# Maximum along the last axis on one core: 17 loads in place of 18, the first of 16 rows, 41 blocks through GpSimd in place of 38, and the last pieces in multiples of 64 columns

## The chip, the core and the metric

The kernel runs on one core of a Trainium2 chip. The engines that matter here are VectorE (DVE in the profile), which reduces along the free dimension; TensorE (PE), used to transpose; ScalarE (ACT), which copies out of PSUM; GpSimd (POOL), which reduces across partitions; and SyncE (SP), whose queue issues the loads. The metric is the device time of one execution in microseconds. The kernel before has a median of 163.62 us in 3 runs (163.6 to 163.85).

## The reference

```python
def setup_inputs():
    batch, seq, dim = 32, 512, 1024
    return {
        "x": np.random.randn(batch, seq, dim).astype(np.float32),
    }

def reference(x: np.ndarray) -> np.ndarray:
    return np.max(x, axis=-1).astype(np.float32)
```

There are 32x512 = 16384 rows of 1024 float32 values, 67.1 MB in all. The output has one value for each row, 64 KB in all.

## The kernel before

The 16384 rows are spread over 128 partitions, so each partition holds 128 rows of 1024 columns. "A row" below always means one such row on all 128 partitions, 512 KB. `BLOCKS` (lines 13 to 16) cuts the 128 rows into loads. The first list is one region of x of 112 rows per partition; the second is a region of 16 rows, 14 of them in loads and 2 in pieces. Each load is one DMA of n rows.

All loads go into a ring of 47 rows in SBUF (`ring`, line 66), whose first 128 columns hold the results (`res`). A load that doesn't fit before the ring's end starts again at row 0. A load is issued from SP's queue (`issue`, line 231) only when every reader of the rows that it overwrites has been written into the program, and on the chip it then waits for those readers. Loads also take turns with eight semaphores, so a load waits for the landing of the load eight places ahead of it.

`PLAN` (lines 31 to 34) is the order of the work, written out by hand. All engines follow it: `in_turn` (line 71) chains each engine's instructions in that order. A step is a letter and a number:

- `d` (direct, line 184): one VectorE maximum over the rows of a load that are VectorE's alone.
- `t` (turn, line 152): a chunk of at most eight 128-column blocks goes another way. TensorE transposes each block into PSUM (`ps`), ScalarE copies them to SBUF (`sb`), and GpSimd's all-reduce takes the maximum over partitions (`top`).
- `b` (back, line 172): TensorE turns one partition of `top` back, a 1x128 transpose for each block, into a small PSUM tile: `got`, one for a load, or for loads in `RANK` the tile `joint`, one for all of them.
- `p` (partial, line 190): VectorE's maximum over the columns of a shared row that GpSimd doesn't take, written beside the values of `b` in the same PSUM tile.
- `m` (merge, line 197): VectorE's maximum over the values of one row in `got` or `joint`, which gives the row's result. `m99` merges all of `joint` and is the last reduction.
- `f` (line 266): VectorE's maximum over one piece.

`SHARED` (line 20) says for a load how many of its rows are shared and how many of their blocks GpSimd takes: `10: (3, 8)` gives GpSimd three whole rows of load 10, `13: (2, 3)` three blocks of two rows each. In all that is 24+6+6+2 = 38 blocks. `RANK` (line 22) lists the loads whose shared rows end in `joint` and sorts them to the end of their region.

`turned` (`sb`), `allr` (`top`) and `psum` (`ps`) have two buffers each (lines 59 to 61), and `joint` is one tile in a pool with one buffer (line 128). The framework puts a semaphore wait between any two instructions of different engines that touch the same tile, one of them writing, in the order of the program; it doesn't compare the columns of `joint`. A third chunk's `top` waits until the first chunk's `b` has read that buffer.

The last two rows come in `PIECES` (line 26): two pieces each, 532+492 and 592+432 columns. The first piece of a row leaves its maximum in the column just before the second piece, whose reduction takes it in. Each piece starts at a multiple of 16 columns in the ring (line 212).

After the first direct maximum come ScalarE's table load and GpSimd's first instruction of the body (lines 252 to 256). The results go out in two stores from ScalarE's queue: 112 columns after the first piece's reduction, 16 after `m99` (lines 270 to 273).

Of the kernel before, what the change touches and what calls it, by code (L numbers as in the profile page):

```python
# [8 lines left out]
F32 = mybir.dt.float32  # L9

BLOCKS = [
    [2, 15, 16, 14, 11, 11, 10, 10, 8, 8, 7],
    [3, 3, 3, 2, 1, 1, 1],
]
RING = 47


SHARED = {10: (3, 8), 13: (2, 3), 14: (2, 3), 17: (1, 2)}  # L20

RANK = {13: 1, 14: 2, 17: 2}

PIECES = [(532, 492), (592, 432)]

PLAN = """
    d0 d1 d2 d3 d4 d5 d6 d7 d8 d9 t0 d10 t1 t2 d11 b0 d12 b1 d13 t3 p13 b2 p14 t4 m10 d15 b3
    d16 p17 t5 f0 b4 f1 f2 b5 f3 m99
""".split()

NOSYNC = mybir.DependencyInfo(mybir.DependencyClass.NoSync, mybir.DependencyReason.DATA)
# [4 lines left out]
def kernel(  # L41
# [11 lines left out]
    N, D = xf.shape  # L53
    C = D // P
    I = N // P
# [10 lines left out]
    ring = once.tile([P, I + RING * D], F32)  # L66
    res = ring[:, :I]
# [9 lines left out]
    def maximum(out, in_):  # L77
        return in_turn("DVE", nc.vector.reduce_max(out=out, in_=in_, axis=X))  # L78
# [15 lines left out]

    loads = []
    views = []
    last = len(PIECES)
    first = at = 0
    for sizes in BLOCKS:
        S = sum(sizes) + last * (sizes is BLOCKS[-1])  # L100
        xb = xf[first * P:(first + S) * P, :].rearrange("(p i) d -> p i d", p=P)
# [5 lines left out]
        b, place = 0, {}  # L107
        for i in sorted(range(len(sizes)), key=lambda i: RANK.get(base + i, 0)):
            place[i] = b
# [8 lines left out]
    assert first == I  # L118
    shared = [SHARED.get(j, (0, C)) for j in range(len(loads))]

    lead = [0 if RANK.get(j) == 3 else n - m for j, ((_, n, _, _), (m, _)) in enumerate(zip(loads, shared))]
    final = [j for j in range(len(loads)) if j in RANK]
    final.sort(key=lambda j: loads[j][3])
# [11 lines left out]
    def rows(j):  # L135
        start, n, _, _ = loads[j]
        return ring[:, I + start * D:I + (start + n) * D].rearrange("p (i d) -> p i d", d=D)
# [4 lines left out]
    def share(j):  # L142
        m, parts = shared[j]
        if j in RANK:
            r = loads[j][3] + lead[j] - col0
            return joint[:, r:r + m, :]
        if j not in fetched:
            got = psmall.tile([P, m, parts + (parts < C)], F32)
            fetched[j] = got
        return fetched[j]  # L150
# [39 lines left out]
    def partial(j):  # L190
        m, parts = shared[j]

        s = width - parts if j in RANK else 1
        maximum(share(j)[:, :, parts:], rows(j)[:, lead[j]:lead[j] + m, parts * P:].rearrange(
# [11 lines left out]
    pieces = []  # L206
    tail = []
    room = I + at * D
    for q in range(len(PIECES[0])):
        for r, widths in enumerate(PIECES):  # L210
            c, w = sum(widths[:q]), widths[q]
            room = -(-(room + 1) // 16) * 16
            pieces.append((ring[:, room:room + w], xb[:, S - last + r, c:c + w]))
            if q:
                tail[-last] = (ring[:, room - 1:room], tail[-last][1])
            tail.append((res[:, I - last + r:I - last + r + 1],
                         ring[:, room - (q > 0):room + w]))
            room += w
    assert room <= I + (at + last + 1) * D


# [81 lines left out]
```

## Time and profile before

| what | value |
|---|---|
| time, median of 3 | 163.62 us |
| span of the profiled execution | 162.0 us |
| around the span, to the median | 1.6 us |
| VectorE busy | 135.3 us (84%) |
| GpSimd, ScalarE, TensorE busy | 16.0, 6.3, 13.6 us |
| mean rate of the DMA engines | 415 GB/s |
| load of 2 rows reduced from | 5.49 us |
| first GpSimd all-reduce | 141.9 us |
| last all-reduce ends | 158.6 us |
| joint maximum ends | 159.68 us |

The span runs from the first to the last instruction of the one execution that was profiled; the device time holds some start and end around it as well. Times in the trace count from the span's start. A line of instructions gives the start, the busy time, engine and line of the code, output and input tile, and in brackets the engine's idle time before it and what ended it. Line 78 is the helper for all VectorE maxima, so its instructions are told apart by their shapes.

### The profile page before, as it was taken

The numbers are of one execution on the slowest core, as the hardware profiler recorded it, in microseconds if no ns is written. First come the engines' busy times: TensorE is split into PE (matmuls) and PEld (weight loads), VectorE is DVE, ScalarE is ACT, GpSimd is POOL, SyncE is SP. The second block draws the span as 40 slices with busy tenths as digits, with TensorE's granted clock in tenths as the row PEclk, the third lists the DMA queues.
The fourth block names the chain that finished last, engine by engine and source line by source line (L and its number), as shares of the span: only waits on it lengthen the run. The fifth ranks groups of instructions, "written<-read, shape, count | busy, mean of one in ns | idle before, by whom it ended". The sixth has DMA issues, their size and how long they took to land.

```text
span 162.0 us, 297 instructions
## 1 busy us (share of the span) xinstructions
PE 13.6 (8%) x76; PEld 11.7 (7%) x76; DVE 135.3 (84%) x33; ACT 6.3 (4%) x7; POOL 16.0 (10%) x11
## 2 busy tenths in 40 slices
PE   0000000000000000000000000000000000772942
PEld 0000000000000000000000000000000000762731
DVE  3500019998399999999999999996999999999994
ACT  0020000000000000000000000000000000241120
POOL 0000000000000000000000000000000000099791
PEclk9999999999999999999999999999999999997555
DMA  5996999599789999898999899799999999999991
GB/s 176 569 486 273 455 502 518 259 518 518 326 354 453 453 405 534 356 534 356 434 456 455 354 486 465 344 486 388 429 478 388 424 418 453 395 431 419 412 386 47
DMA packets 3456, 67.18 MB, mean 415 GB/s; under 512 B 640, under 2 KB 896, under 8 KB 1536
## 3 DMA queue, kind: packets, MB, share of 16 engines
q1 hardware_dynamic: 3168, 67.11, 97.0%
q10 hardware_dynamic: 288, 0.07, 0.2%
HBM read 67.11 MB, written 0.07 MB: 415 GB/s over the span
## 4 chain that ended last, share of the span: by engine, by line
DMA 50%; DVE 47%; SPq 1%; issue 0%; DVEq 0%
DMA ring<-in_x_dram 50%; DVE ring L78 45%; DVE joint L78 2%; SPq L238 1%; DVEq L298 0%
## 5 line engine op out<-in xcount | busy, mean ns | idle before, releaser
L78 DVE TENSOR_REDUCE ring<-ring 128x1 f32<-128x1024 f32 (+13 forms) x20 | 130.0, 6548 | 23.4 <-DMA ring<-in_x_dram 23.3
L168 POOL PARTITION_ALL_REDUCE top<-sb x6 | 15.7, 2657 | 135.0 <-ACT sb L166 134.9
L160 PE MATMUL ps<-ident,ring 128*128 128x128 f32 x38 | 9.1, 424 | 139.9 <-DMA ring<-in_x_dram 139.9
L160 PEld LDWEIGHTS ps<-ident,ring 128*128 128x128 f32 x38 | 7.6, 224 | 139.9 <-issue 139.9
L166 ACT COPY sb<-ps 128x1024 f32<-128x1024 f32 (+2 forms) x6 | 5.0, 834 | 143.2 <-PE ps L160 136.2
L78 DVE TENSOR_REDUCE joint<-ring 128x2 f32<-128x1280 f32 (+1 forms) x3 | 3.9, 1314 | 0.0
L178 PE MATMUL got<-ident,top 1*128 1x1 f32 x24 | 2.7, 228 | 3.7 <-POOL top L168 3.6
L178 PEld LDWEIGHTS got<-ident,top 1*128 1x128 f32 x24 | 2.4, 188 | 4.6 <-POOL top L168 4.6
L178 PE MATMUL joint<-ident,top 1*128 1x1 f32 x14 | 2.0, 245 | 1.9 <-POOL top L168 1.9
L178 PEld LDWEIGHTS joint<-ident,top 1*128 1x128 f32 x14 | 1.7, 210 | 2.7 <-POOL top L168 2.7
L166 ACT ACT_TABLE_LOAD x1 | 1.3, 1283 | 7.9 <-DVE ring L78 7.9
L83 DVE MEMSET ident<- 128x128 f32 x1 | 0.2, 165 | 0.8 <-PEq L287 0.8
L255 POOL MEMSET gate<- 128x1 f32 x1 | 0.1, 99 | 7.4 <-DVE ring L78 7.4
L90 DVE TENSOR_SCALAR rowno<-rowno 32x1 f32<-32x1 f32 x3 | 0.4, 146 | 0.1
L85 DVE TENSOR_TENSOR_SCAN colno<-ident 128x128 f32<-128x128 f32 x1 | 0.4, 424 | 0.0
L92 DVE TENSOR_SCALAR ident<-colno,rowno 128x128 f32<-128x128 f32 x1 | 0.3, 288 | 0.0
L87 DVE STREAM_TRANSPOSE rowno<-colno 128x32 f32<-128x32 f32 x1 | 0.2, 213 | 0.0
L78 DVE TENSOR_REDUCE ring<-got 128x3 f32<-128x24 f32 x1 | 0.2, 173 | 0.0
L78 DVE TENSOR_REDUCE ring<-joint 128x5 f32<-128x20 f32 x1 | 0.2, 169 | 0.0
L287 POOL MEMSET const-float32-0.0<- 128x1 f32 x1 | 0.1, 98 | 0.2 <-issue 0.2
L287 POOL MEMSET const-bfloat16-1.0<- 128x1 bf16 x1 | 0.1, 101 | 0.0
L287 POOL MEMSET const-uint8-127<- 128x1 uint8 x1 | 0.1, 101 | 0.0
(2 smaller groups left out, 0.2 us busy)
## 6 DMA issues: line engine op xcount, KB each, us to landing
ring<-in_x_dram SPq DMA_DIRECT2D x2, 5632.0 KB, 29.9
ring<-in_x_dram SPq DMA_DIRECT2D x2, 5120.0 KB, 36.8
ring<-in_x_dram SPq DMA_DIRECT2D x2, 4096.0 KB, 32.5
ring<-in_x_dram SPq DMA_DIRECT2D x1, 7680.0 KB, 22.5
ring<-in_x_dram SPq DMA_DIRECT2D x1, 7168.0 KB, 57.8
ring<-in_x_dram SPq DMA_DIRECT2D x3, 1536.0 KB, 35.7
ring<-in_x_dram SPq DMA_DIRECT2D x1, 3584.0 KB, 29.2
ring<-in_x_dram SPq DMA_DIRECT2D x2, 1024.0 KB, 17.7
```

Source lines behind the costliest of these rows:

```text
L78: return in_turn("DVE", nc.vector.reduce_max(out=out, in_=in_, axis=X))
L83: in_turn("DVE", nc.vector.memset(ident, 1.0))
L85: in_turn("DVE", nc.vector.tensor_tensor_scan(out=colno, data0=ident, data1=ident, initial=-1.0, op0=ALU.add, op1=ALU.mult))
L87: in_turn("DVE", nc.vector.transpose(out=rowno, in_=colno[:, :32]))
L90: in_turn("DVE", nc.vector.tensor_scalar(out=part, in0=part, scalar1=float(q * 32), scalar2=None, op0=ALU.add))
L92: identity = in_turn("DVE", nc.vector.tensor_scalar(out=ident, in0=colno, scalar1=rowno[:, 0:1], scalar2=None, op0=ALU.is_equal))
L160: in_turn("PE", nc.tensor.transpose(out=ps[:, w:w + P], in_=rows(j)[:, lead[j] + r + i, c * P:(c + 1) * P], identity=ident,))
L166: in_turn("ACT", nc.scalar.copy(out=sb[:, :W], in_=ps[:, :W]))
L168: in_turn("POOL", nc.gpsimd.partition_all_reduce(top[:, :W], sb[:, :W], P, bass_isa.ReduceOp.max))
L178: in_turn("PE", nc.tensor.transpose(out=share(j)[:, r + i, c:c + 1], in_=tops[k][0:1, w:w + P], identity=ident[0:1, 0:1],))
L238: load = nc.sync.dma_start(out=rows(issued), in_=src)
L287: nc = _bacc.Bacc("TRN2", target_bir_lowering=False, num_devices=1)
```

## The change

The rows are cut anew: 16, 12, 14, 13, 13, 11, 10, 9, 7, 7 in the first region and 4, 3, 2, 2, 1, 1, 1 and two rows of pieces in the second. That is 17 loads in place of 18, and the first has 16 rows where it had 2. Loads are renumbered by this: load 8 is the seven-row load just ahead of the last one of the first region, and 10 to 16 are the second region's.

GpSimd takes blocks of seven loads: three blocks of a row of load 8, four blocks of each row in four rows of load 9, three of three rows of load 10, three of two rows of load 12, three of a row of load 14, and two of a row of loads 15 and 16. That makes 3+16+9+6+3+2+2 = 41 blocks in nine chunks (before: 38 in six). Loads 10, 12, 14, 15 and 16 end in `joint`, eight rows of four values; loads 8 and 9 have merges of their own (`m8`, `m9`). In the plan each of these loads has a `p` step, and the `b` steps of loads 10, 12 and 14 now stand between the `p` steps of later loads: `p10`, `p12`, `b3`, `b4`, `p14`, `b5`, `p15`, `p16`, `b6`.

Pieces are written as (row, width) in the order of their issue: 640 of the first row, 576 of the second, 384 of the first, 448 of the second. Widths are multiples of 64 columns, and pieces start at multiples of 64 columns in the ring.

```diff
 BLOCKS = [
-    [2, 15, 16, 14, 11, 11, 10, 10, 8, 8, 7],
-    [3, 3, 3, 2, 1, 1, 1],
+    [16, 12, 14, 13, 13, 11, 10, 9, 7, 7],
+    [4, 3, 2, 2, 1, 1, 1],
 ]
 RING = 47
-SHARED = {10: (3, 8), 13: (2, 3), 14: (2, 3), 17: (1, 2)}
-RANK = {13: 1, 14: 2, 17: 2}
-PIECES = [(532, 492), (592, 432)]
+SHARED = {8: (1, 3), 9: (4, 4), 10: (3, 3), 12: (2, 3), 14: (1, 3), 15: (1, 2), 16: (1, 2)}
+RANK = {10: 1, 12: 2, 14: 2, 15: 2, 16: 2}
+PIECES = [(0, 640), (1, 576), (0, 384), (1, 448)]
 PLAN = """
-    d0 d1 d2 d3 d4 d5 d6 d7 d8 d9 t0 d10 t1 t2 d11 b0 d12 b1 d13 t3 p13 b2 p14 t4 m10 d15 b3
-    d16 p17 t5 f0 b4 f1 f2 b5 f3 m99
+    d0 d1 d2 d3 d4 d5 d6 d7 t0 d8 b0 p8 m8 t1 d9 t2 p9 t3 d10 b1 p10 t4 d11 b2 t5 m9 p12 b3
+    b4 d13 t6 p14 b5 p15 t7 p16 t8 b6 f0 f1 b7 f2 f3 b8 m99
 """.split()
...
-    last = len(PIECES)
+    last = 1 + max(r for r, _ in PIECES)
...
-    for q in range(len(PIECES[0])):
-        for r, widths in enumerate(PIECES):
-            c, w = sum(widths[:q]), widths[q]
-            room = -(-(room + 1) // 16) * 16
-            pieces.append((ring[:, room:room + w], xb[:, S - last + r, c:c + w]))
-            if q:
-                tail[-last] = (ring[:, room - 1:room], tail[-last][1])
-            tail.append((res[:, I - last + r:I - last + r + 1],
-                         ring[:, room - (q > 0):room + w]))
-            room += w
+    done = [0] * last
+    before = [None] * last
+    for r, w in PIECES:
+        c, q = done[r], before[r]
+        room = -(-(room + 1) // 64) * 64
+        pieces.append((ring[:, room:room + w], xb[:, S - last + r, c:c + w]))
+        if q is not None:
+            tail[q] = (ring[:, room - 1:room], tail[q][1])
+        before[r] = len(tail)
+        tail.append((res[:, I - last + r:I - last + r + 1], ring[:, room - (q is not None):room + w]))
+        done[r] = c + w
+        room += w
+    assert done == [D] * last
```

## The prediction

> **What bounds the kernel now.** I read the busy times and the queues first, then who waits for whom, the chain, and the last 25 us instruction by instruction.
>
> The page's busy times and queues:
>
> ```profile
> PE 13.6 (8%) x76; PEld 11.7 (7%) x76; DVE 135.3 (84%) x33; ACT 6.3 (4%) x7; POOL 16.0 (10%) x11
> ...
> q1 hardware_dynamic: 3168, 67.11, 97.0%
> ```
>
> Who waits for whom (us, times, longest):
>
> ```profile
> DVE ring L78 <- DMA ring<-in_x_dram: 23.3, 4, 15.8
> ```
>
> The end of the chain in order of time (start, us):
>
> ```profile
> 110.86 38.94 DMA ring<-in_x_dram
> 149.81 0.02 issue
> 149.83 1.22 DVE ring L78
> ...
> 158.42 0.51 DVE ring L78
> 158.92 0.08 issue
> 159.00 0.59 DVE ring L78
> ```
>
> The load queue keeps the DMA engines busy for 97.0% of the span: the kernel streams 67.11 MB and has no hole in the stream. VectorE (DVE) is the second limit. It loses 23.3 us to loads, nearly all before 43 us, and after 110.8 us never again more than some hundredths: blocks shrink so that each lands just as the one before is reduced. The chain ends in both: the last two pieces (158.42, 159.00) start when they land, and 0.6 us later only the joint maximum and a store follow. So the change can win little and lose whatever makes VectorE wait near the end.
>
> The last stage in the timeline (start, us):
>
> ```profile
> 148.38 1.01 PE L178 MATMUL got<-ident,top 1*128 1x1 f32 x8 [2.55 <-POOL top L168]
> ...
> 152.43 2.50 POOL L168 PARTITION_ALL_REDUCE top<-sb  x1 [0.90 <-ACT sb L166]
> ...
> 154.99 0.79 PE L178 MATMUL joint<-ident,top 1*128 1x1 f32 x6 [0.92 <-POOL top L168]
> 155.05 2.50 POOL L168 PARTITION_ALL_REDUCE top<-sb  x1
> 156.26 0.96 DVE L78 TENSOR_REDUCE joint<-ring 128x2 f32<-128x768 f32 x1
> ...
> 158.66 0.37 PE L178 MATMUL joint<-ident,top 1*128 1x1 f32 x2 [0.25 <-POOL top L168]
> 159.51 0.17 DVE L78 TENSOR_REDUCE ring<-joint 128x5 f32<-128x20 f32 x1
> ```
>
> These are durations I use: a 768-column all-reduce on GpSimd 2.50, six transposes back into the joint tile 0.79, two 0.37, a partial maximum over 768 columns 0.96, the final joint maximum (ends 159.68). In the steps d, t, b, p, m, f below (direct maximum, turn and all-reduce, back, partial, merge, piece) the number is a load's for d, p, m, a chunk's for t, b, a piece's for f.
>
> **Loads.** The two-row load was reduced from 5.49, the load that completes 89 rows from 110.82: 105.33 us for 87 rows and seven loads. Pieces were issued at 142.44, 146.13 and 149.82, each at the landing of a three-row load: 3.69 for three rows and one load. So a row costs 1.2045 us and a load 0.076. One load fewer gains 0.08. Landings in the changed kernel: the first 16 rows at 5.47+14x1.2045 = 22.33; 68 rows (load 4) 85.27; load 12 149.72; loads 14, 15, 16 at 153.48, 154.76, 156.04; pieces 156.87, 157.62, 158.15, 158.75. Before, the same sum gives 158.83 for the last piece. Alignment of the pieces to 64 columns touches 2.7 us of transfers (two rows, four loads); the last piece of before lands as the sum has it, so I take nothing, and 0.1 either way at most.
>
> Does the stream stay full? Load 3 waits for d0 (ends 39.6) while loads up to 53.8 are queued; load 5 for d2 (68.9, queued to 85.3); load 8 for d4 (99.3, to 121.7); load 10 for d5 (111.1, to 138.7); the last piece for load 12 (149.7, 8 us ahead of its turn). The smallest margin is 8 us, so SP's moved waits cost nothing.
>
> **VectorE.** The forms give 17.22 us for 16 rows and 1.21 for one: 1.067 a row plus 0.146, and an instruction with nothing to wait for starts 0.085 before the last one ends, so 0.06 net. Three blocks more on GpSimd take 384 columns off: -0.40. Two reductions more (27 against 25), +0.12; m8, p15 and p16 each wait for the reduction just ahead on VectorE, which costs the overlap and 0.03, about 0.11 each. Sum near zero. The late start at 22.3 is no loss either: VectorE still waits for loads 2, 3 and 4 (1.4, 0.7, 1.7), so its time is set by load 4 at 85.3. From there to the end of p12: 56 whole rows 59.75, 5888 columns of partials 6.14, 14 instructions 0.84, m8's wait 0.11, last end 0.09: 152.25. ScalarE's table load and GpSimd's library step move behind the first reduction, to 39.6; first use is after 130.
>
> **GpSimd and its waits.** Nine all-reduces instead of six: two of 1024 columns (3.3 each), two of 768 (2.50), two of 256 (1.12) and three of 384, which no row shows; between 1.12 and 2.50, by length 1.46. About 18.2 us of work from 131 to the end, so it has room. What it lacks is freedom of order. There are two result buffers (top), so t5 may start only when b3 has read t3's; and b3 writes the joint tile, for which the built order makes it wait until p12 has written the same tile. Then b5 waits for t5, and p15, again a writer of the joint tile, waits for b5. In the kernel before, p17 stood behind b3 alone, which ended at 155.78, before its load landed at 156.1; no partial was held up by TensorE.
>
> That loop, step by step: p12 ends 152.25; b3 starts 0.06 later (as 154.99 follows 154.93) and takes 0.79: 153.10. GpSimd starts 0.09 later (152.43 after ScalarE's 152.34): 153.19, and t5 takes 2.50: 155.69. (t5's own input is ready sooner: load 12 lands at 149.72, six transposes 1.5 and a copy 0.80 as at 149.94 and 151.54, 152.2 with hand-overs.) b5: 0.06+0.79: 156.54. p15 starts about 0.04 later: 156.58. Without it, VectorE would have been ready at: d13 from 152.20 (its load) 2.28, p14 0.73, 155.22, and 0.03: 155.25. Load 15 is there at 154.76. So VectorE stands still 1.33 us, with p16, all four pieces and the final maximum queued behind. The DMA runs on underneath; no cover is left, because VectorE was just on time.
>
> After it: p15 0.96, p16 0.03+0.96, four pieces (640, 576, 385, 449 columns) 0.81+0.75+0.55+0.61, joint maximum 0.18, less five overlaps of 0.085: 4.43. End 161.01, against 159.68: **+1.33**. Close beside it runs GpSimd's own end: p16 ends 158.53, b6 0.06+0.48 (three transposes, 0.106 less for each than six), t8 0.09+1.12, b8 0.06+0.37: 160.71, before the joint maximum's 160.83. With 2.50 for each 384 the loop still stands (t4 would end 153.1, as b3 does) and the end moves by under 0.1.
>
> The span is 162.0 and the median 163.62; the 1.62 around the span and the 2.3 from the last maximum to the span's end stay. 163.62+1.33 = **164.95**.
>
> Terms unknown: b3 and b5 at the faster pace of the first transposes (eight in 0.65 at 145.18, against 1.01 at 148.38 after the granted clock went to 0.5) would give back 0.27 each: 164.4. I take the slow pace, since both lie after 147.6, where all rows of before are slow. The step from TensorE to a GpSimd or VectorE instruction that waits for a buffer is not shown; the nearest hand-overs are 0.03 and 0.14 (landing at 156.13, start 156.27), three such in the loop: -0.1 to +0.3.
>
> The Trainium skill, page "PSUM — Partial Sum Buffer", section on bank collisions, has two engines on one bank and quadrant collide whatever bytes they touch, and asks for semaphores by bank, not by address. By it the waits of b3 and p15 on each other's writes are needed, though they touch different columns: 164.95; if columns alone counted, 163.6. No run here shows a collision; the built order has the waits.
>
> **Rivals.**
> *No stall.* The wait is met in time, because t5 or its neighbours run 1.33 us sooner than summed. Then VectorE ends at 161.01-1.33 = 159.68, as before: 163.6, no change. For it: VectorE's work and the last landing are equal to 0.1. Against: two 2.50 rows, and the order of waits is fixed.
> *A load has a large fixed cost.* The first load was issued at 0.72 and landed at 5.47, of which its two rows are 2.41: 2.34 us fixed. If each load paid that in the stream, one load fewer brings every landing forward by it, the loop with them: 164.95-2.34 = 162.6, faster; it decides from 1.7 us per load on. Against: one- and three-row loads follow each other at 0.076. The Trainium skill, page "DMA: Bandwidth & Descriptors", gives about 2.0 us fixed per DMA; by it the time would be 162.95. The trace's 3.69 us for three rows disagrees for queued loads.
> *A second stall.* GpSimd's end takes over: if waits on buffers cost 0.3 each, t5 and t8 together bring 0.4 to 0.6: 165.4.
>
> **Chances.** Forecast with its unknown terms 0.80 (164.4 to 165.3), second stall 0.11, no stall 0.06, fixed cost 0.03. Range 164.3 to 165.45 leaves about 0.1 to 0.15 out. Bound of what can be told is 0.2%, 0.33 us: slower 0.91, same 0.06, faster 0.03.
>
> **What would show it.** VectorE idle about 1.3 us before a 768-column partial into the joint tile at 156.6, ended by TensorE; GpSimd idle about 1.1 us before the second 768-column all-reduce at 153.2; the last piece landed near 158.75 but reduced only from 160.3; joint maximum near 160.8. Wrong if that partial starts at 155.3, if p12 ends well before 152, or if DMA shows holes.

## The result, and the profile after

The changed kernel takes 165.62 us in the median of four runs (165.59 to 165.65). Against the kernel before on the same chip that is a ratio of 1.0116 [1.0103, 1.013]: slower, by about 1.9 us. The forecast was 164.95 us with a range of 164.3 to 165.45, so the direction was right, and the time lies 0.17 us above the range. The profiled execution took 165.61 us, its span is 163.8.

The page of the changed kernel, with the same two parts as shown of before, busy times and load queue:

```profile
PE 15.7 (10%) x82; PEld 12.7 (8%) x82; DVE 135.1 (82%) x35; ACT 7.1 (4%) x10; POOL 18.1 (11%) x14
...
q1 hardware_dynamic: 3024, 67.11, 95.8%
```

VectorE is busy for 135.1 us where it was 135.3: the three blocks more on GpSimd and the two reductions more nearly cancel, as the prediction had it. The queue moves the same 67.11 MB, and its share falls because the span is longer.

The waits of VectorE, total, times, longest:

```profile
DVE ring L74 <- DMA ring<-in_x_dram: 23.9, 4, 20.2
...
DVE joint L74 <- PE joint L174: 1.5, 1, 1.5
```

The second line is new. Before, VectorE never waited for TensorE.

The last stage in the timeline (start, busy time, instructions; in brackets the idle time before and what ended it):

```profile
151.11 1.48 DVE L74 TENSOR_REDUCE joint<-ring 128x2 f32<-128x1280 f32 x1
152.56 2.29 DVE L74 TENSOR_REDUCE ring<-ring 128x2 f32<-128x2048 f32 x1
...
152.74 1.09 PE L174 MATMUL joint<-ident,top 1*128 1x1 f32 x9 [1.04 <-DVE joint L74]
153.68 3.91 POOL L164 PARTITION_ALL_REDUCE top<-sb  x2 [1.23 <-PE joint L174]
...
154.77 0.82 DVE L74 TENSOR_REDUCE joint<-ring 128x1 f32<-128x640 f32 x1
...
156.23 0.79 PE L174 MATMUL joint<-ident,top 1*128 1x1 f32 x6 [1.40 <-POOL top L164]
...
157.06 1.96 DVE L74 TENSOR_REDUCE joint<-ring 128x2 f32<-128x768 f32 x2 [1.48 <-PE joint L174]
...
158.93 2.46 DVE L74 TENSOR_REDUCE ring<-ring 128x1 f32<-128x640 f32 x4
...
160.90 0.37 PE L174 MATMUL joint<-ident,top 1*128 1x1 f32 x2 [1.07 <-POOL top L164]
161.30 0.19 DVE L74 TENSOR_REDUCE ring<-joint 128x8 f32<-128x32 f32 x1
```

Read the brackets from top to bottom: TensorE's `b3` waits for VectorE (`p12`), GpSimd's `t5` for TensorE, `b5` for GpSimd, and VectorE's `p15` for TensorE. This is the loop of the forecast. VectorE had nothing to do from 155.58, where `p14` ends, to 157.06. Then `p15` and `p16`, four pieces without a gap and the joint maximum, which ends 161.50 where it ended 159.68 before.

The chain that ended last, in order of time, goes through the same loop (start, length, what):

```profile
0.72 21.93 DMA ring<-in_x_dram
22.65 0.02 issue
...
85.59 0.02 issue
85.62 52.66 DVE ring L74 x5
...
151.19 1.41 DVE joint L74
...
152.74 0.78 PE joint L174 x6
...
153.68 2.51 POOL top L164
...
156.23 0.81 PE joint L174 x6
...
157.06 0.97 DVE joint L74
```

The first load landed at 22.65 and load 4 at 85.59. In the chain of before the last two pieces followed their landings; here they don't: the last piece landed at 159.03 and was reduced from 160.78.

### The profile page after: what moved, and what is told of

Read it like the earlier page. It is cut to its first block, busy times and chain, and to the rows that moved or that the text cites. A ratio compares the mean times of both kernels' runs of the same rounds, so it can differ in the third digit from the quotient of the medians.

```text
span 163.8 us, 329 instructions
## 1 busy us (share of the span) xinstructions
PE 15.7 (10%) x82; PEld 12.7 (8%) x82; DVE 135.1 (82%) x35; ACT 7.1 (4%) x10; POOL 18.1 (11%) x14
## 3 DMA queue, kind: packets, MB, share of 16 engines
q1 hardware_dynamic: 3024, 67.11, 95.8%
HBM read 67.11 MB, written 0.07 MB: 410 GB/s over the span
## 4 chain that ended last, share of the span: by engine, by line
DVE 61%; DMA 33%; POOL 2%; issue 2%; PE 1%; POOLq 0%
DVE ring L74 56%; DMA ring<-in_x_dram 33%; DVE joint L74 3%; DVE got L74 2%; POOL top L164 2%; PE joint L174 1%; POOLq L164 0%
## 5 line engine op out<-in xcount | busy, mean ns | idle before, releaser
L74 DVE TENSOR_REDUCE ring<-ring 128x13 f32<-128x13312 f32 (+14 forms) x17 | 124.5, 7361 | 23.9 <-DMA ring<-in_x_dram 23.9
L164 POOL PARTITION_ALL_REDUCE top<-sb x9 | 17.8, 2017 | 103.0 <-ACT sb L162 101.3
L156 PE MATMUL ps<-ident,ring 128*128 128x128 f32 x41 | 10.5, 426 | 137.6 <-DMA ring<-in_x_dram 137.5
L162 ACT COPY sb<-ps 128x384 f32<-128x384 f32 (+3 forms) x9 | 5.8, 644 | 111.5 <-PE ps L156 109.2
L74 DVE TENSOR_REDUCE joint<-ring 128x2 f32<-128x768 f32 (+3 forms) x5 | 6.4, 1273 | 1.5 <-PE joint L174 1.5
L174 PE MATMUL joint<-ident,top 1*128 1x1 f32 x22 | 2.9, 241 | 4.6 <-POOL top L164 2.5
L74 DVE TENSOR_REDUCE got<-ring 128x1 f32<-128x640 f32 (+1 forms) x2 | 3.1, 1552 | 0.0
L174 PEld LDWEIGHTS joint<-ident,top 1*128 1x128 f32 x22 | 2.6, 211 | 5.8 <-POOL top L164 4.4
```

The source lines that it names most:

```text
L156: in_turn("PE", nc.tensor.transpose(out=ps[:, w:w + P], in_=rows(j)[:, lead[j] + r + i, c * P:(c + 1) * P], identity=ident,))
L162: in_turn("ACT", nc.scalar.copy(out=sb[:, :W], in_=ps[:, :W]))
L164: in_turn("POOL", nc.gpsimd.partition_all_reduce(top[:, :W], sb[:, :W], P, bass_isa.ReduceOp.max))
L174: in_turn("PE", nc.tensor.transpose(out=share(j)[:, r + i, c:c + 1], in_=tops[k][0:1, w:w + P], identity=ident[0:1, 0:1],))
```

## The experiments

Two theories were set against each other. The first: the loop of waits costs the time. Rivals: more work or a later end on GpSimd (nine all-reduces, 41 blocks), and the first load of 16 rows. Ratios are to the kernel before on the same chip, where its medians were 163.81 to 163.87.

### The loop taken out, all else kept

```diff
-RANK = {10: 1, 12: 2, 14: 2, 15: 2, 16: 2}
+RANK = {12: 2, 14: 2, 15: 2, 16: 2}
...
-    b4 d13 t6 p14 b5 p15 t7 p16 t8 b6 f0 f1 b7 f2 f3 b8 m99
+    b4 d13 t6 m10 p14 p15 t7 p16 t8 b5 b6 f0 f1 b7 f2 f3 b8 m99
...
-        top = allr.tile([P, D], F32)
+        if W <= 256:
+            top = allr2.tile([P, 256], F32)
+        else:
+            top = allr.tile([P, D], F32)
```

(`allr2` is a second pool with two buffers.) Load 10's values go to a tile of their own, so `b3` no longer stands behind `p12`; `b5` moves behind all three partials and `t8`; and the last two chunks have result buffers of their own.

> The changed kernel with all its 41 blocks and nine chunks, but the waits taken away by other buffers and order: load 10's rows get a tile of their own outside joint, chunks t7 and t8 a result buffer of their own, and p14, p15, p16 stand ahead of b5. Theory (the loop p12, b3, t5, b5, p15 costs VectorE 1.4 us): p15 starts right behind p14 at 155.6, the joint maximum ends near 160.05 in place of 161.50, time 165.62-1.45 = 164.2. Rival (it is the GpSimd work itself, 41 blocks and nine chunks, that makes the end late): 165.6 stays.

Measured: 164.18 us (8 runs), ratio 1.0024 [1.0014, 1.0034]. Its last stage:

```profile
152.71 2.50 POOL L168 PARTITION_ALL_REDUCE top<-sb  x1 [0.24 <-ACT sb L163]
...
154.87 2.81 DVE L75 TENSOR_REDUCE joint<-ring 128x1 f32<-128x640 f32 x3
...
157.58 2.46 DVE L75 TENSOR_REDUCE ring<-ring 128x1 f32<-128x640 f32 x4
...
159.96 0.17 DVE L75 TENSOR_REDUCE ring<-joint 128x5 f32<-128x20 f32 x1
```

`t5` now waits for its own input from ScalarE, and the three partials run in one stretch, with no idle time ahead of any. The joint maximum ends 1.37 us sooner and the time falls by 1.44 (by 1.33 against the second set of runs of the changed kernel, further below). All 41 blocks and nine all-reduces are still there, and so is the first load of 16 rows. So the loop is 1.3 to 1.4 of the 1.7 to 1.9 us by which those two sets are slower than before, and the rival on GpSimd's work falls.

### Each half of it alone

Only the order of one step, `p15` ahead of `b5`:

```diff
-    b4 d13 t6 p14 b5 p15 t7 p16 t8 b6 f0 f1 b7 f2 f3 b8 m99
+    b4 d13 t6 p14 p15 t7 b5 p16 t8 b6 f0 f1 b7 f2 f3 b8 m99
```

> The changed kernel with two steps moved: p15 and t7 ahead of b5, so that p15 no longer waits for b5; all else is as it is, b3 still waits for p12. Theory: p15 starts right behind p14 at 155.6, but b5 now stands behind p15 and p16 behind b5, so the wait shrinks and moves: VectorE idle about 0.9 ahead of p16 (starts 157.5 in place of 158.06), joint maximum 161.0 in place of 161.5, time 165.1. Rival (p15's wait is the whole loss): joint maximum 160.1, time 164.2.

Measured: 164.94 us (4 runs), ratio 1.0064 [1.0049, 1.0079].

```profile
153.52 5.06 POOL L164 PARTITION_ALL_REDUCE top<-sb  x3 [1.23 <-PE joint L174]
...
154.61 1.81 DVE L74 TENSOR_REDUCE joint<-ring 128x1 f32<-128x640 f32 x2
...
156.57 0.77 PE L174 MATMUL joint<-ident,top 1*128 1x1 f32 x6 [0.83 <-DVE joint L74]
...
157.38 0.96 DVE L74 TENSOR_REDUCE joint<-ring 128x2 f32<-128x768 f32 x1 [0.95 <-PE joint L174]
```

`t5` still waits for TensorE and so for `p12`, but `p15` runs at once behind `p14`. Now `b5` waits for `p15` and `p16` waits for `b5`.

Only load 10's own tile (line `RANK` as above, `m10` behind `t6`, `b5` left ahead of `p15`):

```diff
-    b4 d13 t6 p14 b5 p15 t7 p16 t8 b6 f0 f1 b7 f2 f3 b8 m99
+    b4 d13 t6 m10 p14 b5 p15 t7 p16 t8 b6 f0 f1 b7 f2 f3 b8 m99
```

> The changed kernel with load 10's three shared rows in a PSUM tile of their own (one merge more), order otherwise unchanged: b3 needs not wait for p12 any more, so t5 starts at 152.7 in place of 153.7. p15 still waits for b5, and b5 for p14. Theory: b5 starts behind p14 at 155.8, VectorE idle about 0.9 ahead of p15 (starts 156.6 in place of 157.06), joint maximum 161.0, time 165.1. Rival (b3's wait for p12 is the whole cause): joint maximum 160.1, time 164.2.

Measured: 165.09 us (4 runs), ratio 1.0074 [1.0059, 1.0089].

```profile
152.52 2.50 POOL L164 PARTITION_ALL_REDUCE top<-sb  x1 [0.23 <-ACT sb L162]
...
155.64 0.77 PE L174 MATMUL joint<-ident,top 1*128 1x1 f32 x6 [0.98 <-DVE joint L74]
...
156.45 1.96 DVE L74 TENSOR_REDUCE joint<-ring 128x2 f32<-128x768 f32 x2 [0.95 <-PE joint L174]
```

`t5` is now 1.16 us sooner than in the changed kernel (153.68), and yet `p15` gains only 0.61: `b5` waits no longer for GpSimd but for `p14`, which writes the same tile. Both halves leave 0.95 us of idle time, and it is the same thing in both: VectorE's partial ends, about 0.15 later TensorE starts six transposes, 0.77, and 0.04 later VectorE may write the tile again. One `b` of six transposes between two adjacent `p` on one tile costs that much, however early its input is. Neither edit alone takes it away. The first experiment, where it is gone, goes further than the two together: `b5` stands behind all three partials, with the extra result buffers that this needs. Whether that order would have been enough without load 10's own tile was not run.

### The same kind of wait put into the kernel before

```diff
-    d16 p17 t5 f0 b4 f1 f2 b5 f3 m99
+    d16 t5 b4 p17 f0 f1 f2 b5 f3 m99
```

> The kernel before with one step moved: p17 behind t5 and b4, so that it waits for TensorE's transposes of chunk 4 into the joint tile, as p15 waits for b5 in the changed kernel. No work is added. Theory (such a wait late in the plan costs its full length, as nothing covers it): p17 starts behind b4 at 158.45 in place of 156.26, joint maximum about 161.8 in place of 159.68, time 163.62+2.1 = 165.7. Rival (a wait of VectorE there is absorbed by the pieces still landing until 158.9): the end moves by under 0.5, time below 164.1.

Measured: 166.03 us (4 runs), ratio 1.0136 [1.0122, 1.0149].

```profile
157.75 0.80 PE L178 MATMUL joint<-ident,top 1*128 1x1 f32 x6 [0.58 <-POOL top L168]
...
158.58 0.96 DVE L78 TENSOR_REDUCE joint<-ring 128x2 f32<-128x768 f32 x1 [2.04 <-PE joint L178]
...
161.82 0.17 DVE L78 TENSOR_REDUCE ring<-joint 128x5 f32<-128x20 f32 x1
```

2.04 us idle ahead of the last partial make the time 2.22 us longer. So the kernel of before, with its own 38 blocks, 18 loads and pieces, has no cover for such a wait either. Such a wait is enough by itself to cost its length.

### The first load

Three kernels put a larger or smaller first load into the kernel before; two put a start of 2 and 14 rows into the changed kernel, one of them without the loop (the edits of the first experiment, loads renumbered).

```diff
-    [2, 15, 16, 14, 11, 11, 10, 10, 8, 8, 7],
+    [15, 2, 16, 14, 11, 11, 10, 10, 8, 8, 7],
```

> The kernel before with its first two loads in the other order, 15 rows first and then 2: as many loads and bytes. Theory of the late start: the 17 rows and everything after them land about 0.3 us later, and since the tail of this kernel waits for its last pieces, the time is 163.62+0.3 = 163.9. Rival (the start doesn't depend on the first load's size): 163.6. VectorE itself loses nothing: it is idle until 23 us in both.

The others begin with `[16, 1, 16, ...]`, `[8, 9, 16, ...]` and `[1, 16, 16, ...]`:

> The kernel before with its first two loads cut 16+1 in place of 2+15 rows: the first load of the changed kernel, nothing else of it. Theory (a first load of 15 or 16 rows starts the stream 0.2 late, as 15+2 showed, though 8+9 and 1+16 showed nothing clear): time 0.1 to 0.35 above the kernel before. Rival (the start of the stream differs from run to run whatever the first load, and 15+2 was chance): within 0.1.

> The kernel before with its first two loads cut 8+9 in place of 2+15 rows. In the traces so far the last of the 16 DMA engines ends a 2-row first load at 5.47 to 5.58, and a 15- or 16-row one, less its further rows, at 5.64 to 5.82. Theory (the larger the first load's descriptors, the later the last engine is into its stride): 8 rows lie between or with the large ones, last engine at 5.55 to 5.8 after taking off six rows (12.8 to 13.0 as it stands), time 0.05 to 0.25 above the kernel before. Rival (chance from run to run, not size): 5.47 to 5.58, time within 0.1.

> The kernel before with its first two loads cut 1+16 in place of 2+15 rows. Theory of the first load's size: the last engine ends the one row at 4.25 to 4.35, as early as with two rows less one row or up to 0.1 earlier, time 0 to 0.1 below the kernel before. Rival (the size of the first descriptors doesn't matter, or the second load brings the same late start): later landings as with 16 rows first, time 0.2 above.

In the changed kernel:

```diff
-    [16, 12, 14, 13, 13, 11, 10, 9, 7, 7],
+    [2, 14, 12, 14, 13, 13, 11, 10, 9, 7, 7],
```

> The changed kernel with its first load cut into one of 2 rows and one of 14, all else as it is. Theory (a 16-row first load starts the stream 0.32 us late, and every later landing with it): first landing back at 5.47, load of the 4-row block and all behind it 0.25 earlier (0.32 less 0.076 for one load more), joint maximum 161.25, time 165.4. Rival (the 0.32 is chance, or has to do with the stream and not with the first load's size): landings 0.08 later, time 165.7.

> The kernel without the loop (own tile for load 10's rows, own result buffers for t7 and t8, p14 to p16 ahead of b5) and with the first load cut into 2 and 14 rows. If the loop and the late start are all there is, the two gains add: joint maximum about 159.9 against 160.13 without the cut, time 0.2 below that kernel's 164.2 and within 0.2 of the kernel before. Rival (something else of the change, the pieces or the 41 blocks, costs as well): 0.3 or more above the kernel before.

| kernel | first load | time, us | ratio to before | first landing, less 1.2045 for each row over two |
|---|---|---|---|---|
| before | 2 | 163.81 to 163.87 | 1 | 5.47 |
| before, from 15 | 15 | 164.05 (11 runs) | 1.0014 [1.0005, 1.0022] | 5.76 |
| before, from 16 | 16 | 163.95 (11) | 1.001 [1.0001, 1.0019] | 5.66 |
| before, from 8 | 8 | 163.94 (11) | 1.0003 [0.9994, 1.0012] | 5.76 |
| before, from 1 | 1 | 163.90 (11) | 1.0004 [0.9995, 1.0013] | 5.67 |
| changed | 16 | 165.62 (4) | 1.0116 [1.0103, 1.013] | 5.79 |
| changed, from 2 | 2 | 165.51 (4) | 1.0106 [1.0091, 1.0122] | 5.56 |
| changed, no loop | 16 | 164.18 (8) | 1.0024 [1.0014, 1.0034] | 5.82 |
| changed, no loop, from 2 | 2 | 164.03 (10) | 1.0014 [1.0005, 1.0024] | 5.51 |

Each landing is from one profiled execution. A first load of 15 or 16 rows costs the kernel before 0.1 to 0.25 us in time, which the intervals just tell from nothing; 1 and 8 rows can't be told from 2, and neither can a changed kernel that starts from 2 rows from its neighbour that starts from 16. The wait stays when the first load is small again, here in the changed kernel from 2 rows, whose median is that of the second set of runs of the changed kernel (165.51):

```profile
156.88 1.96 DVE L74 TENSOR_REDUCE joint<-ring 128x2 f32<-128x768 f32 x2 [1.48 <-PE joint L174]
```

So the first load is no cause of the loop. What it costs by itself is the 0.1 to 0.25 us above. The theory that a larger first load lands later does not order these starts: the start of 1 row, forecast as early as the small ones, came to 5.67, and that of 8 rows to 5.76, both among the large ones.

### The rest without loop and without the large first load

The changed kernel without the loop, from 2 rows, is still 1.0014 [1.0005, 1.0024], about 0.2 us. Its end:

```profile
152.39 2.29 DVE L75 TENSOR_REDUCE ring<-ring 128x2 f32<-128x2048 f32 x1
...
154.67 2.81 DVE L75 TENSOR_REDUCE joint<-ring 128x1 f32<-128x640 f32 x3
...
157.38 2.46 DVE L75 TENSOR_REDUCE ring<-ring 128x1 f32<-128x640 f32 x4
...
159.75 0.17 DVE L75 TENSOR_REDUCE ring<-joint 128x5 f32<-128x20 f32 x1
```

The two-row load landed at 152.36 and is reduced from 152.39; from there VectorE works without a gap, and the last piece, landed at 158.85, is reduced from 159.23, 0.38 late. Behind that landing, beside the same four pieces, the changed plan leaves VectorE 4224 columns of loads and the plan of before 4096; there the load that completes the same 123 rows landed at 152.29. So the work behind that landing sets the end, and columns that GpSimd takes ahead of it can't bring it forward by more than the 0.03 between landing and start. This is read from the trace and was not tried by itself.

### The pieces

The kernel before with the new form of the pieces alone:

```diff
-PIECES = [(532, 492), (592, 432)]
+PIECES = [(0, 640), (1, 576), (0, 384), (1, 448)]
```

> The kernel before with only the pieces of the changed one: 640, 576, 384, 448 columns at multiples of 64. Theory (their form costs and gains nothing): last landing 158.9 and joint maximum 159.7 as before, time within 0.15 of the kernel before. Rival (columns in multiples of 64 make transfers cheaper): the four pieces land in 2.6 in place of 2.75 us, time 0.1 to 0.2 below.

Measured: 163.81 us (10 runs), ratio 0.9999 [0.9989, 1.0008]. Widths and places in multiples of 64 columns change nothing that can be measured.

### The changed kernel once more

> The changed kernel itself, beside the kernel before on one chip, for a second trace of the same program. Theory: VectorE idle 1.4 to 1.5 ahead of p15, ended by TensorE, in this trace too, since the loop is made of waits; first landing anywhere from 22.4 to 22.7, since the start differs from run to run; time 1.7 to 2.0 above the kernel before. Rival (the first landing at 22.65 is the rule): 22.6 to 22.7 again.

Measured: 165.51 us (4 runs), ratio 1.0103 [1.0089, 1.0117].

```profile
157.00 1.96 DVE L74 TENSOR_REDUCE joint<-ring 128x2 f32<-128x768 f32 x2 [1.48 <-PE joint L174]
```

The idle time is 1.48 again. The first landing was 22.57, 0.08 sooner than in the other profile of the same kernel, and the joint maximum ended 0.07 sooner. The start goes through to the end. These runs alone would lie 0.06 above the range.

No kernel tried is faster than the one before.

## Where the prediction was right, and which terms failed

**The loop: right.** All four waits stand where the forecast put them, each about 0.5 us later: `t5` at 153.68 (forecast 153.19), `b5` at 156.23 (155.75), `p15` at 157.06 (156.58), with 1.48 us of idle time (1.33). Removing it gives back 1.44 us of time.

**VectorE's work: right.** From the landing of load 4 to the end of `p12` the prediction had 152.25-85.27 = 66.98 us (the terms that it prints add up to 66.93); the trace has 152.59-85.59 = 67.00. From the start of `p15` to the end of the joint maximum: 4.43 forecast, 4.44 measured. The all-reduce of 384 columns, estimated at 1.46, took 1.42 to 1.50.

**What made it 165.62 and not 164.95.** The mechanism was right; the step that failed is the size of two terms of the sum, both too small. The larger is "the first 16 rows at 5.47+14x1.2045 = 22.33", which measured 22.65; the second is "the 1.62 around the span", which measured 1.8. The range gave neither of them any width. Either one at its forecast would have brought the time into the range or to its edge. The terms of the miss:

| term | forecast | measured | difference |
|---|---|---|---|
| first landing | 22.33 | 22.65 | +0.32 |
| load 4 to `p12`'s end | 66.98 | 67.00 | +0.02 |
| `p12`'s end to `p15`'s start | 4.33 | 4.47 | +0.14 |
| `p15`'s start to the end of the joint maximum | 4.43 | 4.44 | +0.01 |
| from there to the median | 3.94 | 4.12 | +0.18 |

The landing of load 4, all that VectorE's later work hangs on, was late by the same 0.32 (85.59 for 85.27). The start of 5.47 came from one profile of before and is the earliest of all. Five profiles that begin with two rows landed them at 5.47 to 5.59, mean 5.54; seven that begin with 15 or 16 come out at 5.64 to 5.82 on the same basis, mean 5.72. So of the 0.32, 0.07 was that one early start, 0.18 is the distance between the two means, and 0.07 is that this profile (5.79) was later than its kind. That the size of the first load makes the 0.18 is not shown, since the starts of 1 and 8 rows lie with the large ones; the cause stays open.

In the loop, `b3` starts 0.15 after `p12` (0.06 forecast) and `t5` 0.17 after `b3` (0.09); `b5` starts 0.05 after `t5`'s end and `p15` 0.04 after `b5`. The bound "-0.1 to +0.3" for these hand-overs held. `b3` and `b5` went at the slow pace, as forecast (0.77 and 0.79). That this pace goes with a granted clock of 0.5, as in the profile of before, is not borne out here: the profile of the changed kernel gives the clock as 1.00 throughout, and its eight transposes at 145.45 took 1.01 where those of before at 145.18 took 0.65. What sets the pace is open.

Of the last row, the way from the joint maximum to the end of the span is 2.3 as before, and the rest lies around the span. The 1.62 set the median of three runs against the span of one execution. Wherever time and span of the same execution stand together, in the runs of the experiments, before or changed, they are 1.73 to 1.85 apart. With 1.8 in place of 1.62 the forecast would have been 165.13. The median of 163.62 was low as well: on the other chips it was 163.81 to 163.87.

**The rivals.** *No stall* fell: the waits stand in the trace. *A large fixed cost for each load* fell: with one load fewer, load 4 landed later, not 2.34 us sooner, and from first landing to load 4's it took 62.94 us as the row and load prices give it. *A second stall at GpSimd's end* did not decide, but by nothing: the waits on buffers cost 0.17 each and not 0.3. VectorE may start 0.04 after `b8`, which ended at 161.27, and 0.08 before the end of the last piece, at 161.39; both give 161.30, where the joint maximum starts. With the loop in it, the changed kernel has two paths that end together.

**Costed at nothing and right:** the pieces (0.9999) and SP's moved waits: from the landing of load 4 to that of the last piece the trace has 73.44 us and the sum 73.48, so nothing held the stream up.

## What to carry to other kernels

Where two engines write one tile by turns, the framework's wait is for the whole tile: look at every turn between them on a path without slack, here 0.95 us for one `b` of six transposes between two partials, and 1.48 with an all-reduce in the loop. Breaking one link may only show the next one behind it; a tile of its own for a value, together with all of one engine's writes ahead of the other's, took the turns away here. And a sum hung on the start in one profile has that start's scatter in it: give the range its width, a few tenths here. Take the time around a span from an execution that has both.

## What was not expected of the hardware

The 16 DMA engines don't land a load together. By the traces the landings of a load on the 16 engines lie 0.26 us apart in the profile of before, and 0.33 to 0.7 in all others; most profiles keep their value to within 0.1 from the first load to the last whole one, and the value differs between executions of one kernel (0.55 and 0.43 in the two of the changed kernel). With large first loads it was 0.43 to 0.64, with two rows 0.26 to 0.5, with one row 0.58. The load lands with the slowest engine, so this is part of the scatter of the first landing, and VectorE meets it at every load it waits for.
